# A fourth projection tile by quarters in the opening stage, and expert scratch kept by groups of four blocks and loaded from GpSimd's queue

## The chip, the cores and the metric

The kernel runs on one core of a Trainium2 chip. The metric is the device time of one execution in microseconds (us). All arithmetic is fp32; a product of two fp32 matrices is made of three matmuls on a high and a low half of each factor (hi x hi, hi x lo, lo x hi), and the halves are made on the chip.

## The reference

One layer of a decoder runs on 576 tokens: a prompt of 512 and 8 samples of 8. Width is 2048. Cut to what matters here:

```python
mod = (silu(c) @ w_ada + b_ada).reshape(n, 6, 2048)          # shift1, scale1, gate1, ...
h = rmsnorm(x, norm1_g) * (1 + scale1) + shift1
x_lru, y_gate, sc_b, sc_c, sc_x = split(h @ w_in, ...)       # 5 x 1024 columns
xc = causal_dwconv(x_lru, ...);  rec = rglru(xc + b, ...)    # a scan over time
out_lru = rec * gelu(y_gate)
...                                                          # short conv, two norms, w_out
h2 = rmsnorm(x, norm2_g) * (1 + scale2) + shift2
# peer(h2): 8 heads, each takes 16 of 16384 experts for each token
act = gelu(einsum('td,thkd->thk', h2, expert_u[eidx])) * g
x = x + gate2 * einsum('thk,thkd->td', act, expert_v[eidx])
```

## The kernel before, in words

**Stages, in the trace's time.** To 141 us the modulation (`ada_mm`, L189) streams w_ada in pieces of 1 MB and makes h; projections that can already start run between its pieces. To about 330 us the LRU loop makes one tile of 128 columns of x_lru and one of y_gate for each of i = 0 to 7. The short convolution, the output projection, the second norm and the choice of experts follow to about 1206 us. Experts are then taken in two ways: 80 blocks of 128 experts are computed densely for all tokens, and picks outside these blocks are gathered row by row. In the U stage (1210 to 2205 us) `u_half` multiplies h2 with the blocks (pu, L1400), gelu gives act, and act is written to DRAM scratch `actd`. Beside it the weights of the picks are spread into tiles `stg` by block and token and written to scratch `gd` (L1613). In the V stage (2205 to 3165 us) `v_column` (pv, L1423) multiplies weighted acts with the blocks' rows of V: 80 steps of 4 columns, 12 matmuls each.

**The opening stage.** w_ada comes in for four chunks hc of 512 columns, shift and scale each, and one chunk of the gate: 36 pieces. Modulating a chunk makes a quarter of h's rows, and `first(q, j)` multiplies a sixth of the work of quarter q: tiles x0, x1 (columns 0 and 1 of x_lru) and y0, two halves j of each, 12 matmuls a half. One half stands behind each ada piece from kq == 3 of the next chunk's shift to the end of its scale; the sixth stands at the start of the chunk after that. After the last ada piece (gate, chunk 0) 7 halves are left, and then the loop projects x2, y1, x3, ... with `project`, 96 matmuls each (L139). The order on PE is as written by hand; on other engines a scheduler sets it.

**Scratch.** L = 80 blocks are used in 20 groups sg of SG = 4. `gd[c, partition, block, token]` holds 16 chunks c of 32 tokens; a group needs, in each partition, 16 runs of 4 x 32 floats (512 B). `actd[block, partition, token]` gives a group 4 runs of 2048 B. `load_weights(sg, q)` brings in a quarter of a group's weights (tile gsb, 256 KB) and `load_group` its acts (tile actr, 1 MB), all on ScalarE's queue. `weigh` multiplies them on VectorE (L1352), `halve` makes ahi on ScalarE (L1370) and alo on VectorE (L1374). gsb and actr have one buffer each, so a load waits for the weigh (gsb) or alo (actr) of the group before.

**What sets the order in the V stage.** A table `jobs` hands these out by column: with h_ the column of a group's ahi and hi_at that of the group before (16 columns earlier), the gsb quarters stand at hi_at to hi_at + 3, the actr load at hi_at + 5, weigh at h_ - 3, alo at h_ + 2. SyncE's queue brings in the V blocks (raw, L914, 256 KB), ScalarE makes xhi (L925) and GpSimd xlo (L926) of them. GpSimd also gathers a row of V for each of 128 tokens at a time (v, L1234, 1 MB), up to 5 ahead of use; VectorE adds it up (accB, L1290) and adds the finished columns (acc, L1445). Transfers issued on SyncE and ScalarE take turns at eight completion counters (DMAHW0 to 7), those issued on GpSimd at eight others (DMASW0 to 7): each waits until the one before it on its counter has landed.

Of the kernel before, what the change touches and what calls it, by code (L numbers as in the profile page):

```python
# [5 lines left out]
F32 = mybir.dt.float32  # L6
# [10 lines left out]
KD = 16  # L17
NP = 512
# [62 lines left out]
def build(ctx, tc, A, O, dbg=None):  # L81
# [215 lines left out]
        square_sum(x[:, k, :], k, st, "n1")  # L297
    movs = [(lambda k, a=a, b=b: hv[0][:, k, a:b], lambda k, a=a, b=b: hv[1][:, k, a:b]) for a, b in HALVES]
    LX = 3 + NP + NB * (3 + NS)
    p_early = [pp.tile([128, 2, 512], F32, name=f"pp_x{i}", tag="pp") for i in range(2)]  # L300
    w_early = {}

    def first_weights(q):

        for i, (src, tags) in enumerate(((A["w_in"][1], ("xp", "xc", "hs")), (A["w_in"][KW], ("tr", "ti", "e"))), 1):
            raw, hi, lo = (wk.tile([128, LX], F32, name=f"w{i}{t}{q}", tag=t, bufs=3 - i)[:, :512] for t in tags)
            nc.sync.dma_start(raw, src[q // 2][:, 4 * (q % 2):4 * (q % 2) + 4, :].rearrange("p k c -> p (k c)"))
            S.activation(hi.bitcast(F32R), raw, AF.Copy)
            G.tensor_sub(lo.bitcast(F32R), raw, hi)
            w_early[i, q] = [x.bitcast(F32R).rearrange("p (k c) -> p k c", c=128) for x in (hi, lo)]  # L310

    def first(q, j):

        i, ks = j // 2, range(4 * q + 2 * (j % 2), 4 * q + 2 * (j % 2) + 2)
        if i == 0:
            mm3([p_early[0][:, 0, :HT], p_early[0][:, 1, :HS]], *w_first, movs, ks)
            return
        if q == 0 and j == 4:
            p_early.append([pst.tile([128, 512], F32, name=f"pp_y0{i}", tag="st") for i in range(2)])
        hi, lo = w_early[i, q]  # L320
        outs = [p_early[2][0][:, :HT], p_early[2][1][:, :HS]] if i == 2 else [p_early[1][:, 0, :HT], p_early[1][:, 1, :HS]]
        for k in ks:
            for st, pick in ((hi, 0), (hi, 1), (lo, 0)):
                for o, mv in zip(outs, movs):
                    PE.matmul(o, st[:, k % 4, :], mv[pick](k), start=k == 0 and st is hi and pick == 0,
                              stop=k == KD - 1 and st is lo)

    def scale_x(q):

# [5 lines left out]
    for hc in range(4):  # L335
        for kq in range(4):
            ada_mm(0, hc, kq)
            if hc == 0 and kq == 2:
                spread = norm_stats(st, D, "n1")
            if hc and kq == 0:  # L340
                for p in parts_left:
                    first(*p)
                parts_left = [(hc - 1, j) for j in range(6)]
            if hc and kq == 3:
                first(*parts_left.pop(0))
        ada_out(0, hc)
        for kq in range(4):
            ada_mm(1, hc, kq)
            if parts_left:
                first(*parts_left.pop(0))  # L350
            if hc == 0 and kq == 0:
                R = spread()
                scale_x(0)
        ada_out(1, hc)
        modulate(x, None, 1, 0, 4 * hc, 4, "h")
        if hc == 0:
            w_first = stream_w(A["w_in"][0], "x0")
            for q in range(1, 4):
                scale_x(q)
        first_weights(hc)  # L360
    for kq in range(4):
        ada_mm(2, 0, kq)
    for p in parts_left + [(3, j) for j in range(6)]:
        first(*p)


# [60 lines left out]
    def wt(n, i, b=1):  # L427
        return wk.tile([128, LX], F32, name=f"{n}{i}", tag=n, bufs=b)

    def lru_conv(i, p):  # L430
        xp = wt("xp", i, 2)
        V.memset(xp[:, 0:3], 0.0)
        V.tensor_copy(smp(xp, SO, 3, 0, 3), cst[:, i, :, :])
        S.activation(xp[:, 3:3 + HT], p[:, 0, :HT], AF.Copy)
        S.activation(xp[:, 3 + HT:3 + NP], p[:, 1, :NX], AF.Copy)
        S.activation(smp(xp, SO, 3, 3, 11), s3(p[:, 1, NX:HS]), AF.Copy)
        V.tensor_copy(st_c[:, i, 0, :], xp[:, NP:NP + 3])
        V.tensor_copy(st_c[:, i, 1:, :], smp(xp, SO, 3, 8, 11))
        xc = wt("xc", i, 2)
        cw = lambda k: cols[:, C_CW + k * KW + i:C_CW + k * KW + i + 1]  # L440
        V.tensor_scalar(xc[:, :LN], xp[:, 0:LN], cw(0), cols[:, C_CB + i:C_CB + i + 1], op0=ALU.mult, op1=ALU.add)
        for k in range(1, 4):
            V.scalar_tensor_tensor(xc[:, :LN], xp[:, k:k + LN], cw(k), xc[:, :LN], op0=ALU.mult, op1=ALU.add)
        xcs[i] = xc
# [56 lines left out]

    def sc_x(i, p):
        c = sc_t[i]
        cx = wk.tile([128, LC], F32, name=f"cx{i}", tag="xp", bufs=2)
        V.memset(cx[:, 0:2], 0.0)
        V.tensor_copy(smp(cx, CO, 2, 0, 2), sst[:, i, :, :])
        V.tensor_mul(cx[:, 2:2 + HT], p[:, 0, :HT], c[:, :HT])
        V.tensor_mul(cx[:, 2 + HT:2 + NP], p[:, 1, :NX], c[:, HT:NP])
        V.tensor_mul(smp(cx, CO, 2, 2, 10), s3(p[:, 1, NX:HS]), s3(c[:, NP:]))
        V.tensor_copy(st_s[:, i, 0, :], cx[:, NP:NP + 2])  # L510
        V.tensor_copy(st_s[:, i, 1:, :], smp(cx, CO, 2, 8, 10))
        cv = wk.tile([128, LC], F32, name=f"cv{i}", tag="xc", bufs=2)
# [17 lines left out]
    def ada_turn(n, keep=7):  # L530
# [4 lines left out]
        for _ in range(min(n, len(todo) - keep)):  # L535
            a = todo.pop(0)
            ada_mm(*a)
            if a[2] == 3:
                pend.append(a[:2])
                break  # L540

    gate_act(0, p_early[2])
    lru_conv(0, p_early[0])
    px = p_early[1]
    for i in range(KW):
        if i + 1 < KW:
            lru_conv(i + 1, px)
        if i + 2 < KW:
            px = project(A["w_in"][i + 2], f"x{i + 2}")
            ada_turn(1)  # L550
        lru_gate(i, 0)
        if i + 1 < KW:
            py = project(A["w_in"][KW + i + 1], f"y{i + 1}")
            gate_act(i + 1, [py[:, a, :] for a in range(2)])
        else:
            ada_turn(1)
            pc0 = project(A["w_in"][24], "c0")
        lru_gate(i, 1)
# [153 lines left out]
    V.tensor_copy(outs, words)  # L712
    V.tensor_sub(words[:, 1:], words[:, 1:], outs[:, :KM - 1])
    pickd = dr.tile([NA, 2 * NPK], F32, name="pickd")
    gd = dr.tile([NCH, 128, L, TC], F32, name="gd")
    actd = dr.tile([L, 128, NA], F32, name="actd")
    accd = dr.tile([NA, D], F32, name="accd")
    accs = dr.tile([128, D], F32, name="accs")
    x2d = dr.tile([128, KD, NA], F32, name="x2d")
# [617 lines left out]
    def load_group(sg):  # L1337

        acts[sg] = ep.tile([128, SG, NA], F32, name=f"actr{sg}", tag="actr", bufs=1)
        nc.scalar.dma_start(acts[sg], actd[real(SG * sg):real(SG * sg) + SG].rearrange("i p t -> p i t"))  # L1340

    def load_weights(sg, q):

        if q == 0:
            gsb[sg] = ep.tile([128, NCH, SG * TC], F32, name=f"gsb{sg}", tag="gsb", bufs=1)
        nc.scalar.dma_start(gsb[sg][:, 4 * q:4 * q + 4, :],
                            gd[4 * q:4 * q + 4, :, real(SG * sg):real(SG * sg) + SG, :].rearrange("c p i t -> p c (i t)"))

    def weigh(sg):

# [39 lines left out]
    def u_half(n, i, c):  # L1390
# [213 lines left out]
    def g_out(b, pg):  # L1604
# [5 lines left out]
        if b0 == TC // 4 - 1:  # L1610
            full = stg.pop(c)
            for q in range(0, L, L // 4):
                puts.append(lambda q=q: nc.scalar.dma_start(gd[c][:, q:q + L // 4, :], full[:, q:q + L // 4, :]))  # L1613

    def put(n):
        for f in puts[:n]:
# [28 lines left out]
    for n in range(NU2):  # L1645
# [61 lines left out]
        if n - E0 == 2:  # L1707
            load_group(0)
        for sg, o in ((0, 1), (1, 7)):
            if 0 <= n - E0 - o < 4:  # L1710
                load_weights(sg, n - E0 - o)
        if n - E0 == 6:
            weigh(0)
        if n - E0 == 7:
# [25 lines left out]
    for sg in range(2, L // SG):  # L1740
        use = uses_of[sg * SG]
        free = KQ * (uses_of[(sg - 3) * SG][-1] + 1) if sg >= 3 else 0
        h_ = min(KQ * use[0] - 7, max(free, hi_at + 16))
        assert h_ >= free and h_ >= hi_at + 13, (sg, h_, free, hi_at)
        for j in range(4):
            jobs.setdefault(max(hi_at + j, j), []).append(lambda sg=sg, j=j: load_weights(sg, j))
        jobs.setdefault(max(hi_at + 5, 0), []).append(lambda sg=sg: load_group(sg))
        jobs.setdefault(h_ - 3, []).append(lambda sg=sg: weigh(sg))
        jobs.setdefault(h_, []).append(lambda sg=sg: halve(sg, 0))
        jobs.setdefault(h_ + 2, []).append(lambda sg=sg: halve(sg, 1))  # L1750
        hi_at = h_
# [204 lines left out]
```

## Time and profile before

| what | us |
| --- | --- |
| three runs | 3232.68, 3227.56, 3228.02 (median 3228.02) |
| the profiled execution | 3220.77, its span 3218.9 |
| PE busy | 3040.3 (94%) |
| DVE, POOL, ACT busy | 2216.1, 1730.1, 1039.3 |
| opening stage / U stage / V stage | 0 to 141 / 1210 to 2205 / 2205 to 3165 |

Engines are PE (TensorE), PEld (its weight loads), DVE (VectorE), ACT (ScalarE), POOL (GpSimd) and SP (SyncE). q1 and q10 are the queues of transfers issued by SP and by ACT, q0 that of POOL. A row of waits reads: who waited, for whom, total us, times, longest. A row of windows reads: start and end, length, busy time and instructions of PE, PEld, DVE, ACT and POOL, the granted TensorE clock, the busy share of the 16 DMA engines, GB/s.

### The profile page before, as it was taken

How to read it: one execution, taken by the hardware profiler on the slowest of the kernel's cores; microseconds unless marked ns; L12 is line 12 of the kernel's file. 1: busy time of each engine (PE TensorE's matmuls, PEld its weight loads, DVE VectorE, ACT ScalarE, POOL GpSimd, SP SyncE). 2: the span in 40 equal slices, each digit the busy share in tenths (PEclk: the TensorE clock that was granted, in tenths of full speed). 3: DMA queues.
4: the chain of work that ended last, by engine and by line, in shares of the span. 5: the costliest groups of instructions: out<-in, count | busy, mean ns of one | idle time of the engine just before them, and what ended most of it. 6: DMA issues, size and time to landing. Idle time of an engine off the chain costs nothing.

```text
span 3218.9 us, 52798 instructions
## 1 busy us (share of the span) xinstructions
PE 3040.3 (94%) x20313; PEld 2567.7 (80%) x20313; DVE 2216.1 (69%) x3296; ACT 1039.3 (32%) x1645; POOL 1730.1 (54%) x994
## 2 busy tenths in 40 slices
PE   5999999999989999999999999999999999989997
PEld 2688798899979898887888888877877877777776
DVE  5355521234355797988998998876777897778855
ACT  3243311123232223232656555622222122122122
POOL 2233233344333335666566666666777777577742
PEclk8999999999989999999999999999999999999998
DMA  9834465633332226989879998999999997999964
GB/s 370 300 133 139 156 217 204 210 114 117 130 134 101 73 73 215 314 325 370 340 304 385 389 403 346 372 368 364 399 392 391 389 349 280 357 346 362 363 211 147
DMA packets 300786, 881.13 MB, mean 274 GB/s; under 512 B 37190, under 2 KB 79046, under 8 KB 249062
## 3 DMA queue, kind: packets, MB, share of 16 engines
q1 hardware_dynamic: 161760, 382.48, 33.7%
q0 software_dynamic: 66336, 413.41, 32.4%
q10 hardware_dynamic: 72432, 81.80, 7.3%
q8 instruction: 160, 2.62, 0.3%
q14 instruction: 98, 0.80, 0.1%
HBM read 878.84 MB, written 65.76 MB: 293 GB/s over the span
## 4 chain that ended last, share of the span: by engine, by line
PE 68%; DMA 18%; DVE 6%; issue 3%; POOL 3%; ACT 1%; SPq 0%; ACTq 0%; POOLq 0%; DVEq 0%
PE pu L1400 24%; PE pv L1423 10%; DMA gsb<-gd 7%; PE pp_o L139 6%; DMA actr<-actd 5%; PE pp_s L139 3%; PE pp_c L139 3%; PE pp_x L139 3%; PE qb L139 3%; PE pp_b L139 3%; DMA raw<-vq 3%; PE ada L189 3%; PE pp_y L139 2%; PE qa L139 2%; DMA wa<-w_ada 2%
## 5 line engine op out<-in xcount | busy, mean ns | idle before, releaser
L926 POOL TENSOR_TENSOR xlo<-raw,xhi 128x1024 fp32r<-128x1024 f32 x320 | 786.7, 2467 | 421.4 <-ACT xhi L925 410.3
L925 ACT ACTIVATE xhi<-raw 128x1024 fp32r<-128x1024 f32 x320 | 337.7, 1060 | 856.0 <-PE pv L1423 291.8
L1262 DVE SCALAR_TENSOR_TENSOR u<-u,hT 128x2048 f32<-128x2048 f32 x223 | 504.9, 2283 | 111.7 <-DMA u<-u,rows 111.4
L1290 DVE SCALAR_TENSOR_TENSOR accB<-v,dots,accB 128x2048 f32<-128x2048 f32 x211 | 496.5, 2353 | 114.3 <-DMA v<-v,rows 111.6
L1423 PE MATMUL pv<-ahi,xhi 128*128 128x512 f32 x1280 | 510.4, 399 | 46.0 <-DVE acc L1445 37.4
L1423 PE MATMUL pv<-ahi,xlo 128*128 128x512 f32 x1280 | 507.2, 396 | 15.2 <-POOL xlo L926 15.2
L1400 PE MATMUL pu<-hhi,xhi 128*128 128x512 f32 x1280 | 507.2, 396 | 0.7 <-ACT qt L949 0.7
L1423 PE MATMUL pv<-alo,xhi 128*128 128x512 f32 x1280 | 506.4, 396 | 1.2 <-DVE alo L1374 1.2
L1400 PE MATMUL pu<-hhi,xlo 128*128 128x512 f32 x1280 | 499.5, 390 | 4.8 <-POOL xlo L926 4.8
L1400 PE MATMUL pu<-hlo,xhi 128*128 128x512 f32 x1280 | 499.5, 390 | 0.0
L1423 PEld LDWEIGHTS pv<-ahi,xhi 128*128 128x128 f32 x1280 | 245.2, 192 | 105.5 <-issue 23.1
L1234 POOL DMA_INDIRECT u<-u,rows x223 | 224.7, 1007 | 172.4 <-DVE u L1262 124.9
L1234 POOL DMA_INDIRECT v<-v,rows x223 | 271.6, 1218 | 61.9 <-issue 39.0
L1423 PEld LDWEIGHTS pv<-ahi,xlo 128*128 128x128 f32 x1280 | 245.1, 191 | 72.4 <-POOL xlo L926 20.4
L1400 PEld LDWEIGHTS pu<-hhi,xhi 128*128 128x128 f32 x1280 | 240.7, 188 | 58.0 <-issue 1.7
L1400 PEld LDWEIGHTS pu<-hhi,xlo 128*128 128x128 f32 x1280 | 240.6, 188 | 57.9 <-POOL xlo L926 7.2
L1423 PEld LDWEIGHTS pv<-alo,xhi 128*128 128x128 f32 x1280 | 245.1, 192 | 51.7 <-DVE alo L1374 1.6
L1400 PEld LDWEIGHTS pu<-hlo,xhi 128*128 128x128 f32 x1280 | 240.7, 188 | 47.6
L1595 ACT ACTIVATE op<-op,it 128x128 f32<-128x128 f32 x512 | 155.4, 391 | 2.0 <-issue 0.9
L128 POOL TENSOR_TENSOR wlo_q<-raw_q,whi_q 128x1024 fp32r<-128x1024 f32 x28 | 68.0, 2431 | 149.0 <-ACT whi_q L126 149.0
L189 PE MATMUL ada<-wa,cpad 128*32 128x512 f32 x768 | 108.7, 663 | 40.1 <-DMA wa<-w_ada 40.0
L128 POOL TENSOR_TENSOR wlo_o<-raw_o,whi_o 128x1024 fp32r<-128x1024 f32 x32 | 77.7, 2427 | 115.9 <-ACT whi_o L126 115.9
(503 smaller groups left out, 5543.1 us busy)
## 6 DMA issues: line engine op xcount, KB each, us to landing
wa<-w_ada SPq DMA_DIRECT2D x96, 1024.0 KB
raw<-ut SPq DMA_DIRECT2D x160, 512.0 KB
raw<-vq SPq DMA_DIRECT2D x320, 256.0 KB
gd<-stg ACTq DMA_DIRECT2D x64, 320.0 KB
gsb<-gd ACTq DMA_DIRECT2D x80, 256.0 KB
actd<-act ACTq DMA_DIRECT2D x76, 256.0 KB
actr<-actd ACTq DMA_DIRECT2D x19, 1024.0 KB
raw_o<-w_out SPq DMA_DIRECT2D x32, 512.0 KB
```

The lines of the kernel that those rows point to most:

```text
L128: lo_engine(share).tensor_sub(lo, raw, r32(hi))
L139: PE.matmul(o, st, mv[pick](k), start=first, stop=last)
L189: PE.matmul(acc[32 * g:32 * g + 32, :], cpad[:, 4 * kq + g, :], w[:, g, :], start=kq == 0, stop=kq == 3)
L925: S.activation(hi, raw, AF.Copy)
L926: G.tensor_sub(lo, raw, r32(hi))
L1234: G.indirect_dma_start(out=out, out_offset=None, in_=src, in_offset=bass.IndirectOffsetOnAxis(ap=idx, axis=0), bounds_check=NE * 128 - 1, ...
L1262: V.scalar_tensor_tensor(r, r, 1.0, st["h"], op0=ALU.mult, op1=ALU.mult, accum_out=dots[i][:, j:j + 1])
L1290: V.scalar_tensor_tensor(st["a"], r, dots[i][:, j:j + 1], st["a"], op0=ALU.mult, op1=ALU.add)
L1400: PE.matmul(pu, st[:, kk, :], movA[mv](k), start=k == 0 and a == 0, stop=k == KD - 1 and a == 2)
L1423: PE.matmul(pv, st, mv, start=first and j == 0 and a == 0, stop=last and not end and j == SG - 1 and a == 2)
L1595: S.activation(ops[:, j0 + j, :], ops[:, j0 + j, :], AF.Copy, scale=it[2][:, b * 4 + j:b * 4 + j + 1])
```

## The change

**A, the opening stage.** A fourth tile, x2, joins: a quarter has 8 halves. One stands behind every ada piece from kq == 3 on into the next chunk, so that after the last piece 3 + 8 = 11 are left. The x2 weights come in by quarters of 256 KB on SyncE (tags w3r, w3h, w3l) ahead of the following ada pieces. The first 256 columns of x0 and x1 share one PSUM bank and those of y0 and x2 another; `clear` zeroes each with one matmul, and ScalarE copies them out (`both`) at the loop's start. The loop no longer projects x2: y1 comes first, and `lru_in` (copies out of PSUM) is cut from `lru_conv`.

**B, the scratch.** gd is laid out as [group][partition][chunk][4 x 32 tokens] and actd as [group][partition][block][token]: a group is 8192 B in one run in each partition. Each is loaded by one 1 MB transfer on GpSimd's queue, gsb at hi_at and actr at hi_at + 4; weigh moves to h_ - 2. The stores of gd (64 of 320 KB on ScalarE's queue) now consist of runs of 512 B instead of 2560 B; those of actd keep runs of 2048 B.

```diff
+    def clear(bank):
+        PE.matmul(bank, ident, none.to_broadcast([128, 512]), start=True, stop=False)
...
-        for i, (src, tags) in enumerate(((A["w_in"][1], ("xp", "xc", "hs")), (A["w_in"][KW], ("tr", "ti", "e"))), 1):
+        for i, (src, tags, b) in enumerate(((A["w_in"][1], ("xp", "xc", "hs"), (3, 2, 2)), (A["w_in"][KW], ("tr", "ti", "e"), (1, 1, 1)),
+                                            (A["w_in"][2], ("w3r", "w3h", "w3l"), (2, 1, 1))), 1):
...
-            if hc and kq == 0:
-                for p in parts_left:
-                    first(*p)
-                parts_left = [(hc - 1, j) for j in range(6)]
             if hc and kq == 3:
+                parts_left = [(hc - 1, j) for j in range(8)]
+            if parts_left:
                 first(*parts_left.pop(0))
...
-    for p in parts_left + [(3, j) for j in range(6)]:
+    for p in parts_left + [(3, j) for j in range(8)]:
...
+    for i, bank in ((0, pe_[1][:, 0, :]), (2, p_yx)):
+        both = wk.tile([128, 512], F32, name=f"both{i}", tag="w3r", bufs=2)
+        S.activation(both, bank, AF.Copy)
...
-        if i + 2 < KW:
+        if i and i + 2 < KW:
             px = project(A["w_in"][i + 2], f"x{i + 2}")
             ada_turn(1)
...
-    gd = dr.tile([NCH, 128, L, TC], F32, name="gd")
-    actd = dr.tile([L, 128, NA], F32, name="actd")
+    gd = dr.tile([L // SG, 128, NCH, SG * TC], F32, name="gd")
+    actd = dr.tile([L // SG, 128, SG, NA], F32, name="actd")
...
-        nc.scalar.dma_start(acts[sg], actd[real(SG * sg):real(SG * sg) + SG].rearrange("i p t -> p i t"))
-    def load_weights(sg, q):
-        if q == 0:
-            gsb[sg] = ep.tile([128, NCH, SG * TC], F32, name=f"gsb{sg}", tag="gsb", bufs=1)
-        nc.scalar.dma_start(gsb[sg][:, 4 * q:4 * q + 4, :],
-                            gd[4 * q:4 * q + 4, :, real(SG * sg):real(SG * sg) + SG, :].rearrange("c p i t -> p c (i t)"))
+        G.dma_start(acts[sg], actd[real_sg[sg]])
+    def load_weights(sg):
+        gsb[sg] = ep.tile([128, NCH, SG * TC], F32, name=f"gsb{sg}", tag="gsb", bufs=1)
+        G.dma_start(gsb[sg], gd[real_sg[sg]])
...
-        for j in range(4):
-            jobs.setdefault(max(hi_at + j, j), []).append(lambda sg=sg, j=j: load_weights(sg, j))
-        jobs.setdefault(max(hi_at + 5, 0), []).append(lambda sg=sg: load_group(sg))
-        jobs.setdefault(h_ - 3, []).append(lambda sg=sg: weigh(sg))
+        jobs.setdefault(max(hi_at, 2), []).append(lambda sg=sg: load_weights(sg))
+        jobs.setdefault(hi_at + 4, []).append(lambda sg=sg: load_group(sg))
+        jobs.setdefault(h_ - 2, []).append(lambda sg=sg: weigh(sg))
```

The first place is PE in the opening stage, at the shift pieces kq = 1 to 3 of chunk 3 (wa_3_1 to wa_3_3, four matmuls a row). Before, these pieces follow one another, and the first half of the next quarter (x0, tile pp_x) comes behind the last:

```order
L189 MATMUL ada_3_655<-wa_3_1_674,cpad 32x512 x4
L189 MATMUL ada_3_655<-wa_3_2_680,cpad 32x512 x4
L189 MATMUL ada_3_655<-wa_3_3_686,cpad 32x512 x4
L139 MATMUL pp_x_164<-hhi,whi_x_1_291 128x256
L139 MATMUL pp_x_164<-hhi,whi_x_1_291 128x320
```

After, a half of the x2 tile (12 matmuls with weights w3h and w3l; its outputs are printed as pp_y_432 and pp_y_433, the banks it shares) stands behind the first of these pieces, and another behind the second:

```order
L189 MATMUL ada_3_701<-wa_3_1_720,cpad 32x512 x4
L340 MATMUL pp_y_432<-hhi,w3w3h_490 128x256
L340 MATMUL pp_y_433<-hhi,w3w3h_490 128x320
L340 MATMUL pp_y_432<-hlo,w3w3h_490 128x256
L340 MATMUL pp_y_433<-hlo,w3w3h_490 128x320
L340 MATMUL pp_y_432<-hhi,w3w3l_491 128x256
L340 MATMUL pp_y_433<-hhi,w3w3l_491 128x320
```

Pieces that had nothing behind them have a half behind them now; a chunk has eight halves between its pieces where it had six.

The second place is POOL in the V stage, at the first pass over the gathers (v_30 to v_35). Before:

```order
L1234 DMA v_30_22726<-v,rows_8671 128x2048
L926 TENSOR_TENSOR xlo_22745<-raw_22465,xhi_22744 128x1024
L926 TENSOR_TENSOR xlo_22749<-raw_22563,xhi_22748 128x1024
L1234 DMA v_31_22783<-v,rows_8671 128x2048
L1234 DMA v_32_22820<-v,rows_8671 128x2048
L926 TENSOR_TENSOR xlo_22841<-raw_22572,xhi_22840 128x1024
L926 TENSOR_TENSOR xlo_22845<-raw_22653,xhi_22844 128x1024
L1234 DMA v_33_22866<-v,rows_8671 128x2048
L1234 DMA v_34_22885<-v,rows_8671 128x2048
L1234 DMA v_35_22918<-v,rows_8671 128x2048
```

After:

```order
L1265 DMA v_30_22732<-v,rows_8690 128x2048
L957 TENSOR_TENSOR xlo_22752<-raw_22475,xhi_22751 128x1024
L957 TENSOR_TENSOR xlo_22756<-raw_22570,xhi_22755 128x1024
L1265 DMA v_31_22790<-v,rows_8690 128x2048
L1376 DMA gsb_22798<-gd 128x2048
L1265 DMA v_32_22826<-v,rows_8690 128x2048
L957 TENSOR_TENSOR xlo_22846<-raw_22579,xhi_22845 128x1024
L957 TENSOR_TENSOR xlo_22850<-raw_22660,xhi_22849 128x1024
L1265 DMA v_33_22871<-v,rows_8690 128x2048
L1265 DMA v_34_22889<-v,rows_8690 128x2048
L1371 DMA actr_22894<-actd 128x2048
L1265 DMA v_35_22922<-v,rows_8690 128x2048
```

The two loads of a group have come into POOL's row between the gathers: gsb ahead of gather 32, actr ahead of gather 35. The same loads before, on ACT:

```order
L1443 ACTIVATE acc<-pv_12_22676 128x512
L1370 ACTIVATE ahi_22788<-actr_22599 128x2048
L1346 DMA gsb_22791<-gd 128x4x128
L1443 ACTIVATE acc<-pv_13_22694 128x512
L1346 DMA gsb_22791<-gd 128x4x128
L1443 ACTIVATE acc<-pv_14_22713 128x512
L1346 DMA gsb_22791<-gd 128x4x128
L1443 ACTIVATE acc<-pv_15_22731 128x512
L925 ACTIVATE xhi_22840<-raw_22572 128x1024
L925 ACTIVATE xhi_22844<-raw_22653 128x1024
L1346 DMA gsb_22791<-gd 128x4x128
L1340 DMA actr_22903<-actd 128x4x512
```

After, ACT's row in the V stage has no transfer in it, only xhi, ahi and the first columns' acc.

More of the change, by code (lines that the diff above doesn't have):

```diff
@@ L299, in build @@
     LX = 3 + NP + NB * (3 + NS)
-    p_early = [pp.tile([128, 2, 512], F32, name=f"pp_x{i}", tag="pp") for i in range(2)]
+    pe_ = [pp.tile([128, 2, 512], F32, name=f"pp_x{i}", tag="pp") for i in range(2)]
+    p_early = [(pe_[1][:, 0, HT * i:HT * i + HT], pe_[0][:, i, :HS]) for i in range(2)]
     w_early = {}
+    none = c1.tile([128, 1], F32, name="none")
+    V.memset(none, 0.0)
+    def clear(bank):
+        PE.matmul(bank, ident, none.to_broadcast([128, 512]), start=True, stop=False)
     def first_weights(q):
-        for i, (src, tags) in enumerate(((A["w_in"][1], ("xp", "xc", "hs")), (A["w_in"][KW], ("tr", "ti", "e"))), 1):
-            raw, hi, lo = (wk.tile([128, LX], F32, name=f"w{i}{t}{q}", tag=t, bufs=3 - i)[:, :512] for t in tags)
+        for i, (src, tags, b) in enumerate(((A["w_in"][1], ("xp", "xc", "hs"), (3, 2, 2)), (A["w_in"][KW], ("tr", "ti", "e"), (1, 1, 1)),
+                                            (A["w_in"][2], ("w3r", "w3h", "w3l"), (2, 1, 1))), 1):
+            raw, hi, lo = (wk.tile([128, LX if i < 3 else 512], F32, name=f"w{i}{t}{q}", tag=t, bufs=c)[:, :512] for t, c in zip(tags, b))
             nc.sync.dma_start(raw, src[q // 2][:, 4 * (q % 2):4 * (q % 2) + 4, :].rearrange("p k c -> p (k c)"))
@@ L310, in first_weights @@
             w_early[i, q] = [x.bitcast(F32R).rearrange("p (k c) -> p k c", c=128) for x in (hi, lo)]
+    p_yx = None
     def first(q, j):
+        nonlocal p_yx
         i, ks = j // 2, range(4 * q + 2 * (j % 2), 4 * q + 2 * (j % 2) + 2)
-        if i == 0:
-            mm3([p_early[0][:, 0, :HT], p_early[0][:, 1, :HS]], *w_first, movs, ks)
-            return
+        if q == 0 and j == 0:
+            clear(pe_[1][:, 0, :])
         if q == 0 and j == 4:
-            p_early.append([pst.tile([128, 512], F32, name=f"pp_y0{i}", tag="st") for i in range(2)])
-        hi, lo = w_early[i, q]
-        outs = [p_early[2][0][:, :HT], p_early[2][1][:, :HS]] if i == 2 else [p_early[1][:, 0, :HT], p_early[1][:, 1, :HS]]
+            a, b = [pst.tile([128, 512], F32, name=f"pp_y0{i}", tag="st") for i in range(2)]
+            p_early.extend([(a[:, :HT], pe_[1][:, 1, :HS]), (a[:, HT:2 * HT], b[:, :HS])])
+            clear(a)
+            p_yx = a
         for k in ks:
[L323 to L326, printed above, removed]
+            if i:
+                wh, wl = (w[:, k % 4, :] for w in w_early[i, q])
+            else:
+                wh, wl = (w[k // 8][:, k % 8, :] for w in w_first)
+            for st, pick in ((wh, 0), (wh, 1), (wl, 0)):
+                for z, (o, mv) in enumerate(zip(p_early[i], movs)):
+                    PE.matmul(o, st, mv[pick](k), start=z == 1 and k == 0 and st is wh and pick == 0,
+                              stop=k == KD - 1 and st is wl and z + i % 2 > 0)
     def scale_x(q):
@@ L428, in wt, with lru_in, lru_conv @@
         return wk.tile([128, LX], F32, name=f"{n}{i}", tag=n, bufs=b)
-    def lru_conv(i, p):
-        xp = wt("xp", i, 2)
+    xps = {}
+    def lru_in(i, p):
+        xps[i] = xp = wt("xp", i, 3)
         V.memset(xp[:, 0:3], 0.0)
         V.tensor_copy(smp(xp, SO, 3, 0, 3), cst[:, i, :, :])
-        S.activation(xp[:, 3:3 + HT], p[:, 0, :HT], AF.Copy)
-        S.activation(xp[:, 3 + HT:3 + NP], p[:, 1, :NX], AF.Copy)
-        S.activation(smp(xp, SO, 3, 3, 11), s3(p[:, 1, NX:HS]), AF.Copy)
+        S.activation(xp[:, 3:3 + HT], p[0][:, :HT], AF.Copy)
+        S.activation(xp[:, 3 + HT:3 + NP], p[1][:, :NX], AF.Copy)
+        S.activation(smp(xp, SO, 3, 3, 11), s3(p[1][:, NX:HS]), AF.Copy)
+    def lru_conv(i):
+        xp = xps.pop(i)
         V.tensor_copy(st_c[:, i, 0, :], xp[:, NP:NP + 3])
@@ L503, in sc_x @@
         c = sc_t[i]
-        cx = wk.tile([128, LC], F32, name=f"cx{i}", tag="xp", bufs=2)
+        cx = wk.tile([128, LC], F32, name=f"cx{i}", tag="xp", bufs=3)
         V.memset(cx[:, 0:2], 0.0)
@@ L540, in ada_turn @@
                 break
+    for i, bank in ((0, pe_[1][:, 0, :]), (2, p_yx)):
+        both = wk.tile([128, 512], F32, name=f"both{i}", tag="w3r", bufs=2)
+        S.activation(both, bank, AF.Copy)
+        for j in range(2):
+            p_early[i + j] = both[:, j * HT:j * HT + HT], p_early[i + j][1]
+    lru_in(0, p_early[0])
+    lru_in(1, p_early[1])
     gate_act(0, p_early[2])
-    lru_conv(0, p_early[0])
-    px = p_early[1]
+    lru_in(2, p_early[3])
+    lru_conv(0)
     for i in range(KW):
+        if 1 < i < KW - 1:
+            lru_in(i + 1, [px[:, a, :] for a in range(2)])
         if i + 1 < KW:
-            lru_conv(i + 1, px)
-        if i + 2 < KW:
+            lru_conv(i + 1)
+        if i and i + 2 < KW:
             px = project(A["w_in"][i + 2], f"x{i + 2}")
             ada_turn(1)
-        lru_gate(i, 0)
+        if i:
+            lru_gate(i, 0)
         if i + 1 < KW:
@@ L554, in build @@
             gate_act(i + 1, [py[:, a, :] for a in range(2)])
+            if not i:
+                ada_turn(1)
+                lru_gate(0, 0)
         else:
@@ L1404, in u_half @@
             if i < L - SG:
-                nc.scalar.dma_start(actd[i], act)
+                nc.scalar.dma_start(actd[i // SG, :, i % SG, :], act)
             else:
@@ L1612, in g_out @@
             for q in range(0, L, L // 4):
-                puts.append(lambda q=q: nc.scalar.dma_start(gd[c][:, q:q + L // 4, :], full[:, q:q + L // 4, :]))
+                puts.append(lambda q=q: nc.scalar.dma_start(
+                    gd[q // SG:(q + L // 4) // SG, :, c, :].rearrange("s p x -> p s x"),
+                    full[:, q:q + L // 4, :].rearrange("p (s i) t -> p s (i t)", i=SG)))
     def put(n):
@@ L1709, in build @@
         for sg, o in ((0, 1), (1, 7)):
-            if 0 <= n - E0 - o < 4:
-                load_weights(sg, n - E0 - o)
+            if n - E0 == o:
+                load_weights(sg)
         if n - E0 == 6:
```

## The prediction

> **What bounds the kernel now.** I read the page from the top: engines, slices, then the chain.
>
> ```profile
> PE 3040.3 (94%) x20313; PEld 2567.7 (80%) x20313; DVE 2216.1 (69%) x3296; ACT 1039.3 (32%) x1645; POOL 1730.1 (54%) x994
> DMA  9834465633332226989879998999999997999964
> ```
>
> PE is busy 94% of the span, so all that any edit can win is its idle 6% or matmuls taken away. The DMA engines are full in two places: the first slices and nearly all of the last half. The windows of the opening stage, U and V come next.
>
> ```profile
> 104.00:128.00 24.00, 19.48 (x141) 10.42 (x133) 7.91 (x19) 5.17 (x8) 4.36 (x3) 0.95 1.05 398
> 1550.00:2120.00 570.00, 570.00 (x5969) 461.99 (x5968) 506.04 (x691) 333.76 (x729) 362.89 (x242) 1.00 0.92 364
> 2250.00:3050.00 800.00, 746.84 (x3196) 607.46 (x3196) 644.06 (x358) 177.50 (x166) 585.14 (x342) 0.98 0.97 364
> ```
>
> In U, PE never stops and DMA has 8% to spare. In V, DMA is 97% busy and PE lacks 53 of 800 us: V is where transfers set the pace. The waits there (2225 to 3080) and the chain say which.
>
> ```profile
> ACT xhi L925 <- DMA raw<-vq: 221.0, 46, 14.6
> POOL xlo L926 <- ACT xhi L925: 163.4, 54, 12.7
> DVE accB L1290 <- DMA v<-v,rows: 107.3, 58, 8.8
> PE pv L1423 <- DVE acc L1445: 37.4, 14, 7.5
> DVE actr L1352 <- DMA actr<-actd: 32.2, 6, 9.8
> PE pv L1423 <- POOL xlo L926: 13.5, 10, 2.7
> SPq L914 <- DMA gsb<-gd: 345.4, 45, 19.4
> 2185.85 26.65 DMA gsb<-gd
> 2314.18 25.89 DMA actr<-actd
> 2831.83 38.14 DMA gsb<-gd
> ```
>
> PE waits mostly for VectorE's acc, and VectorE for rows of V and for a group's loads. The last wait row is the telling one: SP's loads of V blocks stand 345 us behind gsb loads, because both take turns at the same eight completion counters. So a scratch load that takes 26 to 38 us holds the blocks, these hold xhi, xlo and PE.
>
> **B, the V stage.** Removed in the 800-us window: 68 loads of gsb and 17 of actr on ACT's queue. Added: as many MB on POOL's queue, one transfer each.
>
> ```profile
> q0 software_dynamic: 29751, 186.72, 58.6%
> q1 hardware_dynamic: 37712, 68.67, 24.2%
> q10 hardware_dynamic: 44404, 35.05, 13.9%
> gsb<-gd ACTq DMA_DIRECT2D x68, 256.0 KB
> actr<-actd ACTq DMA_DIRECT2D x17, 1024.0 KB
> v<-v,rows POOLq DMA_INDIRECT x201, 10.8
> ```
>
> q10 carries nothing but these. It takes 13.9% for 35.05 MB, q0 58.6% for 186.72 MB, in runs of 8192 B (a gathered row), as the scratch will be. At q0's price 35.05 MB take 35.05 x 58.6 / 186.72 = 11.0%; 2.9% of 800 us, 23 us of all 16 engines' time, fall away. DMA work goes from 776 to 753 us; PE's 3196 matmuls start 0.228 us apart when nothing holds them (the rows below, five steps in 1.14 us): 729. DMA stays the longer one and V follows it: **-23**. Bounds: 0 if run length is not what made q10 dear, -47 (800 to 753) if DMA's 3% of idleness goes too.
>
> ```profile
> 2204.73 0.39 PE L1423 MATMUL pv<-ahi,xhi 128*128 128x512 f32 x1
> 2205.87 0.39 PE L1423 MATMUL pv<-ahi,xlo 128*128 128x512 f32 x1
> ```
>
> A rule gives the first bound less: the Trainium skill, "DMA: Bandwidth & Descriptors", section "Why small descriptors are slow (HBM only)", has a fixed overhead of some 3 cycles a packet; at the 850 MHz of its section "Where 436 GB/s comes from" 39,000 packets fewer would be an estimated 9 us over 16 engines, and the sum would be 14 us less of a gain. The row's 2.9% is kept, since it is measured on these very transfers.
>
> Part of the idle 3% is of the change's own making: with no transfer of ACT left in V, SP's blocks no longer queue behind gsb or actr at a counter (345 us of waits), and ACT's xhi no longer behind a held issue. Of the idle 24 us I give a quarter, **-6**; 0 if SP then waits for xlo's buffers instead, -24 at most.
>
> What it costs on POOL: an issue like accs<-v, plus the 0.3 us gap that its neighbours show.
>
> ```profile
> L1296 POOL DMA_DIRECT2D accs<-v x1 | 0.6, 582 | 0.0
> L926 POOL TENSOR_TENSOR xlo<-raw,xhi 128x1024 fp32r<-128x1024 f32 x134 | 334.4, 2512 | 154.0 <-ACT xhi L925 152.1 <-DMA raw<-vq 1.1
> ```
>
> 34 loads x 0.9 us = 30 us, inside the 152 us in which POOL stands waiting for xhi; where it is not idle, behind the load are xlo and then PE. I take a tenth: **+3** (0 to +15). The loads wait for VectorE: gsb for the last weigh, actr for the last alo, and gathers and xlo queue behind them. At the place where each load will stand, the weigh or alo is over in the trace in most groups, by some 16 us on average; the closest pair is this:
>
> ```profile
> 2400.68 1.00 POOL L1234 DMA_INDIRECT v<-v,rows  x1 [0.16 <-issue]
> 2403.14 2.29 DVE L1374 TENSOR_TENSOR alo<-actr,ahi 128x2048 fp32r<-128x2048 f32 x1
> ```
>
> There a load would hold POOL from 2401 to 2405.4, 4 us. I sum about 15 us of holds over 34 loads, also inside the 152. Gathers behind a load land up to 3.5 us later (1 MB at 300 to 364 GB/s), with five ahead of use; before, the same bytes ran beside them on another queue, so the rows come no later on the whole. Moving weigh one column on costs nothing while it has been waiting for its loads (32.2 us above).
>
> **B, the start of V.** PE's wait here ends with the first gsb loads:
>
> ```profile
> 2209.83 0.50 PE L1423 MATMUL pv<-ahi,xhi 128*128 128x512 f32 x1 [3.58 <-ACT xhi L925]
> 2212.62 1.29 DVE L1361 TENSOR_TENSOR actr<-act,gsb 128x512 f32<-128x512 f32 x2 [8.75 <-DMA gsb<-gd]
> ```
>
> VectorE waits 8.75 us for group 1's weights, and ACT's xhi stands behind. The chain's 26.65 us for that load becomes one transfer behind a few gathers (10.8 us). **-4**: the 3.58 and some of what follows at a cold clock; 0 to -8, the bound being VectorE's wait.
>
> **B, the stores in U.** 64 stores of 320 KB change from 2560-B to 512-B runs.
>
> ```profile
> q10 hardware_dynamic: 10817, 22.56, 14.4%
> gd<-stg ACTq DMA_DIRECT2D x42, 320.0 KB
> ```
>
> In 1600 to 2000 (rows above) q10 paid 14.4% of 400 us for 22.56 MB, 41 engine-us a MB; in V, mixed 512 and 2048 B, 51; with actr at U's 41 to 45, gsb's own 512-B runs cost about 57. (57 - 41) x 21 MB / 16 = 21 us more DMA work, against 8% of U's 700 us of stores, 56 us. PE has no wait in U to lengthen: **+2** (0 to +15).
>
> **A.** The trace's chain where the pieces end, and the loop's start:
>
> ```profile
> 119.57 6.45 DMA wa<-w_ada
> 126.06 1.93 PE ada L189 x8
> 138.04 3.12 PE pp_y L325 x24
> 141.17 12.80 PE pp_x L139 x96
> 156.56 12.99 PE pp_y L139 x96
> ```
>
> Removed: x2's 12.80 us. Added: two halves' worth of tail twice over, 11 instead of 7, four at 3.12 / 2 = 1.56: 6.2 us. The rest of x2 goes between pieces, where the chain waits for wa anyway. But 1.05 MB of x2 weights now run ahead of the last piece in a stage where DMA is full (share 1.05, 398 GB/s): 2.6 us. Two clears, matmuls of 512 columns as in ada, are 0.5. ACT's copies precede y1's end by more than 6 us in the new order. -12.8 + 6.2 + 2.6 + 0.5 = -3.5, rounded to **-4**. Bounds: -7 if the last piece is not later (the x2 weights then no longer compete in the loop), -1 if the pieces, now a half behind each, also pay PE time where wa came early.
>
> **The sum.** -23 - 6 + 3 - 4 + 2 - 4 = -32 against the profiled 3220.77, which lies 7.3 us under the median of the runs shown, 3228.0. On the median: 3228 - 32 = **3196**.
>
> **Rivals.**
> 1. *The scratch was hidden anyway.* VectorE still waits for rows of V (107.3 us), the gathers share their queue with the scratch, and PE's 37.4 us for acc stay. For it: DVE is busy 644 of 800 us, POOL 585, and both are chained to rows. Against: SP's 345 us and the loads on the chain. Then A and half of V's start remain: 3228 - 6 = 3222, about 3218 to 3232.
> 2. *Slower: POOL held at the loads.* A load that waits for VectorE holds the gathers and xlo behind it. POOL's 152 us of idleness over 34 loads are 4.5 us a load: from there on the hold decides. At 7 us a load, (7 + 0.9) x 34 = 269, less 152 = 117 us of POOL's time. If half of it reaches PE through a late xlo, +58, less the 35 gained in the other terms: 3251. For it: weigh and alo lengthen beside POOL's work, and gathers beside them,
>
> ```profile
> L1352 DVE TENSOR_TENSOR actr<-actr,gsb 128x2048 f32<-128x2048 f32 x16 | 50.9, 3181 | 46.5 <-DMA actr<-actd 32.2 <-DMA raw<-vq 14.2
> 2292.66 5.90 DVE L1352 TENSOR_TENSOR actr<-actr,gsb 128x2048 f32<-128x2048 f32 x1
> 2354.18 2.87 POOL L1234 DMA_INDIRECT v<-v,rows  x1 [0.16 <-issue]
> 2357.36 1.00 POOL L1234 DMA_INDIRECT v<-v,rows  x1 [0.30 <-issue]
> ```
>
> a weigh 5.90 us against a mean of 3.18, a gather 2.87 against 1.00. Against: the load waits for just that weigh or alo, which is then over. The Trainium skill, "SBUF — State Buffer", section "SBUF: two separate sides", warns of this: a transfer issued from GpSimd gets no descriptors while VectorE holds the shared port, and it says to issue from SP or ACT. The trace agrees as far as that one gather goes.
> 3. *More: the pipeline frees itself.* Blocks come early, weighs never wait, V runs at DMA's 753 us: -47 instead of -29, and V's start -8: 3228 - 60 = 3172.
> 4. *U becomes DMA-bound* by the short stores, from the point where they cost more than 8%: +15 and late first loads: 3212.
>
> **How the numbers follow.** My forecast 0.54 (3180 to 3212), rival 1 0.17, rival 2 0.11, rival 3 0.12, rival 4 0.06. A measurement here can tell 0.2%, 6.5 us, from no change: same is 3221.5 to 3234.5. Faster: 0.54 + 0.12 + 0.06 and a third of rival 1, 0.77; same: two thirds of rival 1 and a bit of rival 2's near end, 0.13; slower 0.10. The range 3168 to 3230 leaves out rival 2, the top of rival 1 and the far end of rival 3.
>
> **What would show it.** In V: no transfers on q10, q0's share near 69%, DMA share still 0.95 or more over a V stage some 30 us shorter; no weigh waiting for actr; SP waiting for xlo, not gsb; POOL's waits for VectorE at the loads about 15 us in all. At the start: PE's first wait under 2 us. In U: PE still without idleness, DMA share 0.95. In the opening: 11 halves in 17 us behind the last piece, y1 at about 152.5 instead of 156.56. The prediction is wrong if POOL's loads or gathers show waits for VectorE above 100 us, if accB's waits for rows grow by more than the weighs' shrink, or if the queue's price for scratch on q0 is no lower than it was on q10.

## The result, and the profile after

The changed kernel takes 3241.98 us (median of 6 runs, 3237.29 to 3252.43), the kernel before 3227.79 (6 runs): a ratio of 1.0053, 95% interval 1.0034 to 1.0071. The forecast was 3196, faster; it is slower by half a percent. The profiled execution took 3237.29 (span 3235.5), that of before 3220.77 (span 3218.9): 16.6 us between the spans, and the stages show where. The bounds are the first pu and pv matmuls and the last row of pv in the two traces (in that of before it starts at 3190.8, so V reaches beyond 3165). Two executions at a much lower granted clock, one of the kernel before (3551.95 us, clock 0.80) and one of e3 (8659.67, clock 0.64), are left out of every ratio and range.

| stage, us | before | after | change | forecast |
| --- | --- | --- | --- | --- |
| start of U (all that comes before) | 1209.8 | 1206.4 | -3.4 | -4 |
| U | 994.9 | 1047.4 | +52.5 | +2 |
| V, to its last row of pv | 986.1 | 953.0 | -33.1 | -30 (-23, -6, +3, -4) |

The start of U and V came out near their forecasts. U lost more than both gained. First the page and the windows of after: U's stretch, and 800 us of V.

```profile
PE 3049.9 (94%) x20317; PEld 2574.8 (80%) x20317; DVE 2214.5 (68%) x3297; ACT 1041.5 (32%) x1649; POOL 1737.4 (54%) x1035
1550.00:2170.00 620.00, 585.77 (x5950) 469.96 (x5949) 508.39 (x692) 332.27 (x723) 364.48 (x243) 0.98 0.90 337
2300.00:3100.00 800.00, 766.19 (x3319) 627.42 (x3318) 669.81 (x376) 185.59 (x172) 607.71 (x383) 0.99 0.94 367
```

In V, PE now does 3319 matmuls in 800 us where it did 3196. In U, where the window of before shows no idleness, it is idle for 34 of 620 us, with the DMA share at 0.90, below the 0.92 of before: U isn't short of transfer time on the whole. What PE waits for in U, in the rows of waits, and what ACT does at one such place, in the timeline (ACTq is ACT's issuing of transfers):

```profile
PE gbank L1630 <- ACT stg L1637: 16.2, 3, 8.9
PE gx L1630 <- issue: 11.5, 28, 0.5
PE gx L1630 <- ACT act L1432: 5.9, 1, 5.9
2043.49 11.43 ACTq L1642 DMA_DIRECT2D gd<-stg  x2
2055.02 0.70 ACT L1637 ACTIVATE stg<-gbank 128x320 f32<-128x320 f32 x1 [10.49 <-issue]
2170.40 17.02 DMA gd<-stg
```

Two stores of gd hold ACT's queue for 11.4 us; the copy into stg behind them comes 10.5 us late, and PE's next gbank matmuls wait for it. The last row is from the chain, at the end of U: it now runs through a store. The rows of the store's line in both traces give the issue's duration (smallest, median, largest, ns), 64 stores each:

```profile
L1613 ACTq DMA_DIRECT2D gd<-stg x64: 326/444/1387, 1555.0 to 2117.2; - x64
L1642 ACTq DMA_DIRECT2D gd<-stg x64: 366/616/10516, 1551.6 to 2172.3; - x64
```

V after, in the queues' rows (2300 to 3100), the waits (2275 to 3090) and PE's first wait in the timeline:

```profile
q0 software_dynamic: 34980, 220.95, 68.9%
q1 hardware_dynamic: 39744, 72.37, 25.2%
SPq L945 <- POOL xlo L957: 409.9, 138, 13.5
DVE accB L1321 <- DMA v<-v,rows: 116.3, 82, 5.0
PE pv L1452 <- DVE acc L1474: 27.6, 15, 7.1
POOL gsb L1376 <- DVE actr L1381: 4.5, 2, 2.8
2257.19 0.50 PE L1452 MATMUL pv<-ahi,xlo 128*128 128x512 f32 x1 [1.41 <-POOL xlo L957]
```

q10 is gone and q0 has 68.9%, as forecast; the DMA share is 0.94, where 0.95 or more was expected. SP no longer waits for gsb; it waits for xlo to free its buffers. No weigh waits for actr. POOL's holds at the loads are 4.5 us in all. PE's first wait in V is 1.41 us, where it was 3.58.

### The profile page after: what moved, and what is told of

Read it like the earlier page. It is cut to its first block, busy times and chain, and to the rows that moved or that the text cites. A ratio compares the mean times of both kernels' runs of the same rounds, so it can differ in the third digit from the quotient of the medians.

```text
span 3235.5 us, 52712 instructions
## 1 busy us (share of the span) xinstructions
PE 3049.9 (94%) x20317; PEld 2574.8 (80%) x20317; DVE 2214.5 (68%) x3297; ACT 1041.5 (32%) x1649; POOL 1737.4 (54%) x1035
## 4 chain that ended last, share of the span: by engine, by line
PE 73%; DMA 11%; DVE 7%; issue 3%; POOL 2%; ACTq 1%; ACT 1%; SPq 0%; POOLq 0%; DVEq 0%
PE pu L1429 23%; PE pv L1452 16%; PE pp_o L139 6%; DMA v<-v,rows 4%; PE pp_s L139 3%; PE pp_c L139 3%; PE qb L139 3%; PE pp_b L139 3%; PE ada L189 2%; PE pp_y L139 2%; PE qa L139 2%; DMA raw<-vq 2%; PE pp_x L139 2%; DVE accB L1321 2%; DMA wa<-w_ada 2%
## 5 line engine op out<-in xcount | busy, mean ns | idle before, releaser
L1265 POOL DMA_INDIRECT v<-v,rows x223 | 258.2, 1158 | 67.8 <-issue 42.0
L1432 ACT ACTIVATE act<-pu 128x512 f32<-128x512 f32 x80 | 47.8, 597 | 290.2 <-PE pu L1429 269.5
```

The costliest lines, as they stand in the source:

```text
L1265: G.indirect_dma_start(out=out, out_offset=None, in_=src, in_offset=bass.IndirectOffsetOnAxis(ap=idx, axis=0), bounds_check=NE * 128 - 1, ...
```

## The experiments

The runs e1 to e4, e5 to e8 and e9 to e12 were made together in three groups, each on another chip, where the kernel before took 3228.06, 3214.67 and 3213.08 us; each ratio is against the kernel before of its own group. A U or V given is that of the one profiled execution. How far these lengths vary is shown by one kernel on two chips (e6 and e12: U 999.8 and 1002.1, V 952.7 and 946.9) and by e4, whose V, with nothing of V edited, is 6.5 us under that of before. So V's differences of 6 us between groups tell nothing.

One theory after the result: the stores' 512-B runs cost U its time. The rivals: part A, the loads on GpSimd's queue, or the transfers' sheer work. And for V's gain: run length, or the freed counters.

**e4_a_only.** Part A's edits alone on the kernel before.

> Part A alone on the kernel before. If A is worth what the changed kernel's stage bounds say, the U stage begins 3.4 us earlier than before (1206.4 against 1209.8), U and V keep the lengths of before (995 and 986 us, to the last pv matmul), and the time is 3 to 4 us below that of the kernel before. Rival: the 3.4 us were a matter of that one profile, and U begins at 1209 or later.

Measured: 3223.01 against 3228.06 (ratio 0.9989, 0.9973 to 1.0005). U starts at 1207.2, V is 979.6. But U is 1008.9, 14 us more than before, with waits that no earlier profile had:

```profile
PE gx L1632 <- issue: 9.4, 23, 0.5
```

The gain of 3 us was there, the length of U was not as expected. The waits turn up in the profiles of e1 to e4, which ran together, and in that of after, and in none of e5 to e12; see the last section.

**e1_old_gd.** The changed kernel with the old layout of gd.

```diff
-    gd = dr.tile([L // SG, 128, NCH, SG * TC], F32, name="gd")
+    gd = dr.tile([NCH, 128, L, TC], F32, name="gd")
-        G.dma_start(gsb[sg], gd[real_sg[sg]])
+        G.dma_start(gsb[sg], gd[:, :, real(SG * sg):real(SG * sg) + SG, :].rearrange("c p i t -> p c (i t)"))
...
+                puts.append(lambda q=q: nc.scalar.dma_start(gd[c][:, q:q + L // 4, :], full[:, q:q + L // 4, :]))
```

> The changed kernel with gd as before ([chunk][partition][block][token]): its 64 stores are 2560-B runs again, and a group's weights still come as one 1 MB transfer on GpSimd's queue, now of 512-B runs. Theory 1 (the stores' five times as many packets are what U lost): U is back from 1047 to 995 to 1000 us. V: if the 33 us won came from freeing the eight counters and ACT's queue, V stays at 953 to 960; if they came from the saved transfer work, of which only the acts' 5 us are left, V is about 975 to 980. Time 3228 - 4 - 30 = 3194 by the first, 3215 by the second. Rival (U was lost to the loads on GpSimd's queue or to part A): U stays near 1047.

Measured: 3212.45 (0.9958, 0.9943 to 0.9973), U 1010.3, V 969.3. U is that of e4, which holds the old stores too: the stores' layout cost 37 us (1047.4 less 1010.3; 39 against e3, of the same group), and the loads on GpSimd's queue cost U nothing. V lies between the two values expected.

**e2_spaced.** `put(1)` for `put(2)`.

> The changed kernel with at most one store of gd issued in each half of the U stage instead of two (put(1) for put(2)): same packets, same bytes. Theory 1a (a burst of stores fills ACT's queue, and ScalarE stands until it drains): ACT's issue time for gd falls from 116 us to under 50, U from 1047 to about 1005 to 1015. Theory 1b (a store of 640 packets costs that issue time whatever stands before it) and theory 2 (the transfer engines run out of time in U): U stays within 10 us of 1047.

Measured: 3217.58 (0.9964, 0.9951 to 0.9978), U 1031.2, V 952.2. ACT's issues of the stores take 38 us in all instead of 98 (their durations in the trace of after sum to 97.8, not to the 116 expected), as theory 1a has it, but U got back only 16 us, between the two theories. The standing had moved to what is issued behind them on ACT's queue, the writes of act:

```profile
2046.53 8.48 ACTq L1434 DMA_DIRECT2D actd<-act  x1
2055.11 1.06 ACT L956 ACTIVATE xhi<-raw 128x1024 fp32r<-128x1024 f32 x1 [8.61 <-issue]
```

In the stretch in which stores are issued these writes take 56 us to issue here, 28 in after and 15 before. With the stores ACT's queue is held 94 us here, 125 in after and 45 before. SP's loads of U blocks also wait 81 us for stores at a shared counter, where they waited 5.

**e3_loads_act.** `G.dma_start` replaced by `nc.scalar.dma_start` in load_group and load_weights.

> The changed kernel with both loads of a group on ACT's queue again, one transfer of 1 MB in 8192-B runs each, at the new places. U keeps its 1047 us. V: if the saved transfer work made V's gain, V stays near 955 to 960; if the freed counters and ACT's queue made it, V returns to 975 to 985. Time about 3242 by the first, 3265 by the second.

Measured: 3239.35 (1.0035, 1.0011 to 1.0058), U 1049.5, V 947.3. V's whole gain is there with both loads on ACT's queue and the eight counters shared as before. Its queues (2300 to 3100):

```profile
q0 software_dynamic: 30082, 185.29, 57.5%
q10 hardware_dynamic: 4896, 35.65, 11.3%
```

**e5_stores_sp.** The stores on SP's queue (`nc.sync.dma_start` in puts).

> The changed kernel with the 64 stores of gd issued on SP's queue instead of ACT's: same packets, bytes and places. Theory 1 (U lost its 37 us to ScalarE standing at the issue of these stores, with stg and xhi behind them): U falls from 1047 to 1005 to 1015, the issue time moves to SP, and V keeps its 953: about 3205. Theory 2 (transfer engines or DRAM are too slow for 512-B stores): U stays above 1035. Rival 3: SP now stands instead, its loads of the U blocks (raw) come late and PE waits for xhi: U 1020 to 1040.

Measured: 3238.3 against 3214.67 (1.0071, 1.0046 to 1.0096), U 1045.0, V 945.2. ACT issues no store and U is as long. PE's waits in U: a copy into stg comes late, and PE waits for it.

```profile
PE pu L1429 <- ACT stg L1637: 30.0, 8, 12.8
PE gbank L1630 <- ACT stg L1637: 9.3, 4, 5.1
DMA to landing us min/median/max: 5.3/17.7/27.4
```

The third row is from the store's line, from issue to landing, of the 35 stores whose landing the trace has; e8, the kernel before, has 4.7/14.6/18.9 for nine. stg has two buffers, but no late store held one of them here: by the packets in the trace, a chunk's stores had all ended 17 us or more before the first copy into the same buffer. The timeline shows another reason, first on SP, then on ACT, then on PE; the last two rows are ACT's waits for U blocks, before (1550 to 2205) and here (1550 to 2250):

```profile
1757.44 21.82 SPq L940 DMA_DIRECT2D raw<-ut  x4
1769.20 1.06 ACT L956 ACTIVATE xhi<-raw 128x1024 fp32r<-128x1024 f32 x1 [10.58 <-DMA raw<-ut]
1770.16 0.71 ACT L1637 ACTIVATE stg<-gbank 128x320 f32<-128x320 f32 x1
1771.49 0.50 PE L1429 MATMUL pu<-hhi,xhi 128*128 128x512 f32 x1 [2.63 <-ACT stg L1637]
ACT xhi L925 <- DMA raw<-ut: 30.0, 9, 7.6
ACT xhi L956 <- DMA raw<-ut: 134.8, 23, 19.5
```

Now SP stands: in the stretch of the stores its issues of them take 120 us and those of the U blocks among them 173, where those took 29 before. The blocks come late, ACT's xhi waits for them, the copies into stg stand behind xhi in ACT's order, and PE waits for the copies. That is rival 3 of the expectation, at a higher price. Theory 1 falls as far as it names ScalarE; what it says of the engine that issues stays.

**e6_stores_pool.** The stores on GpSimd's queue (`G.dma_start` in puts).

> The changed kernel with the stores of gd on GpSimd's queue, among the gathers. Theory 1: U falls to 1005 to 1020, since POOL has idle time in U; the gathers behind a store land later and VectorE waits more for rows of u. Rival: 640 packets a store written by GpSimd cost it more than its idle time, xlo comes late and U stays at 1030 or more.

Measured: 3187.3 (0.9901, 0.9880 to 0.9923), U 999.8, V 952.7. The same stores into the same layout cost U 5 us instead of 45. The rows of the store's line, and of the window's queues (1550 to 2120):

```profile
L1642 POOL DMA_DIRECT2D gd<-stg x64: 860/914/943, 1553.9 to 2125.7; - x64
DMA to landing us min/median/max: 7.1/10.7/12.6
q0 software_dynamic: 27443, 149.96, 65.7%
q10 hardware_dynamic: 6345, 11.55, 5.3%
```

POOL issues a store in 0.91 us, and the ten landings that the trace has come after 10.7 us, the latest after 12.6. No write of act and no U block takes more than 0.4 us to issue. Where 40,960 packets of 512 B left ACT's queue, the trace of e6 has packets of 4096 B on q0 (5216 of them in U, 96 of which stand there before too): the trace lists eight runs as one packet.

**e7_old_gd_act.** e1 with both loads on ACT's queue.

> Run e1 with both loads of a group on ACT's queue: gd in the old layout with 512-B load runs, actd in the new one, one transfer each. Beside e1 (V 969) it shows what GpSimd's queue alone is worth in V, beside e3 (V 947) what the length of gsb's runs is worth. If the queue matters (freed counters), V is 980 or more; if only run lengths and the number of transfers do, V is 965 to 972. U as in e1, 1010.

Measured: 3202.74 (0.9957, 0.9934 to 0.9981), U 999.5, V 963.7. The queue alone is worth nothing that shows in V (e1 969.3, this 963.7); gsb's run length is worth 16 us (963.7 against e3's 947.3 with the loads on ACT's queue, e1's 969.3 against after's 953.0 with them on GpSimd's). Its q10 (2250 to 3050) costs what that of before did:

```profile
q10 hardware_dynamic: 37536, 35.65, 13.7%
SPq L945 <- DMA gsb<-gd: 235.1, 12, 30.5
```

SP stands at gsb for 235 us here, and V is shorter than before by 22 us all the same.

**e8_before.** The kernel before, once more.

> The kernel before, unchanged, for a second profile of it. Its 27 times so far lie between 3217 and 3233 us, and the first profile (3220.8) is among the low ones; the two kernels that hold part A and the old stores had 23 waits of 0.4 us in the gx matmuls of U, 9.4 us, and U of 1009 to 1010 us. If these waits belong to single executions, they turn up here with a time above 3225; if they belong to part A, this profile has none and U is 995.

Measured: 3220.82, U 994.0, V 988.1, no waits at gx. The profile of before was no chance: U and V are within 2 us of it.

**e9_stores_two.** The four stores of a chunk in turn on ACT's and SP's queue.

```diff
-                puts.append(lambda q=q: nc.scalar.dma_start(
+                puts.append(lambda q=q: (nc.sync if q % (L // 2) else nc.scalar).dma_start(
```

> The changed kernel with the four stores of a chunk issued in turn on ACT's and on SP's queue. In runs e3 and e5 each 512-B run was a packet of its own on these queues, in e6 the same stores went out from GpSimd in 4096-B packets, and U was 1045 to 1050 there and 1000 here. Theory 4 (a queue gets one packet a turn on each transfer engine, so 40 packets a store and engine wait 40 turns): with two queues a chunk's 160 turns run side by side, the stores land earlier, and U falls to 1015 to 1030. Rival (the stores' bytes or DRAM's handling of 512-B runs set the time, whatever the queue): U stays at 1045.

Measured: 3212.63 against 3213.08 (1.0000, 0.9986 to 1.0013), U 1021.7, V 953.4. With two queues half of the loss is gone, in the range that theory 4 gave; the bytes and their 512-B runs are the same. Its reason is not borne out: a store lands after 3.7/19.1/28.8 us here, no earlier than in e5. No issue of a store takes longer than 1.5 us now, and the U blocks on SP's queue take 59 us to issue, where e5 has 173; but ACT's xhi still waits 131 us for them, and PE for stg (16.2 and 11.0 us):

```profile
L1642 SPq DMA_DIRECT2D gd<-stg x32: 382/405/1504, 1543.9 to 2134.4; - x32
L1642 ACTq DMA_DIRECT2D gd<-stg x32: 377/377/775, 1549.7 to 2142.0; - x32
```

**e10_b_pool, e11_pool_act, e12_pool_again.** e6 without part A; e6 with the loads on ACT's queue; e6 again.

> Part B alone with the stores on GpSimd's queue (run e6 without part A): U starts at 1208 to 1210 instead of 1205 to 1206, U is 995 to 1000, V 953; the time is 2 to 4 us above run e12 of this call. Rival: A costs as much elsewhere as it saves, and the two are equal.

> Run e6 with the loads of gsb and actr on ACT's queue, stores on GpSimd's. V followed the transfer engines' work in all runs so far (share 0.96), and that is the same here: V 945 to 955, time within 6 us of e12. If the eight counters that SP and ACT share cost something, V is 960 or more.

> Run e6 again, on this call's chip: U 1000 and V 953 again, about 27 us (0.9%) under the kernel before.

Measured, against 3213.08: e10 3187.74 (0.9927, 0.9902 to 0.9952), e11 3181.88 (0.9903, 0.9882 to 0.9923), e12 3186.35 (0.9917, 0.9898 to 0.9937). U starts at 1210.2 without A and at 1206.2 and 1205.5 with it; U is 1000 to 1002 and V 945 to 947 in all three. A's 4 to 5 us at U's start are plain in the traces and too small for the times (1.4 us, inside the intervals). The lowest median is that of e11 (both parts, loads on ACT's queue, stores on GpSimd's), about 1% under the kernel before; its interval overlaps those of e10 and e12.

## Why the prediction was wrong, point by point

**The step that failed: "B, the stores in U", +2 (0 to +15).** It priced the stores as transfer work only. That work was sized about right: in the U window q10 went from 14.2% of 570 us to 15.7% of 630, 81 to 99 us, +18 where 21 was forecast, and the DMA share even fell. What it left out is the issue: "PE has no wait in U to lengthen" looked at PE alone and took the engine that issues as free. With 640 packets instead of 128 in a store, the issues of stores and of acts hold ACT for 125 us where they held it for 45, up to 10.5 us at a time. ACT's copies into stg and its xhi stand behind the issue in ACT's order, and PE behind the copies. With the stores on SP's queue the same happens by way of the U blocks (e5). U lost 37 us (after against e1, both with the waits at gx) to 45 us (e5 against e6, both without). The other 14 or so of the 52 go with the waits at gx, which are themselves 9 to 12 us: e4 has them, and a U 14 us longer, with the old stores, and e6 and e7 hold part A without them.

**Rival 4** had the right place, the short stores, and the wrong mechanism and size: it asked for U to become short of DMA time, at +15. U was not; its share was 0.90.

**What makes them slow.** Shown: not the layout or the bytes (e6: 1000), not ScalarE as the one that issues (e5: 1045), but many short packets on one hardware queue, whose issuing engine then stands (e9, two queues: 1022; e2, spaced: 1031). A buffer of stg held by a late store is not it: by the packets in the traces, a chunk's stores end at least 14.5 us before the first copy into the same buffer in before, 6.6 in after, 17.0 in e5 and 16.8 in e9; only e2, which spaces them out, comes closer, to 0.4. The trace's packets take 27 ns for 512 B, 103 for 2560, 171 for 4096 and 320 to 331 for 8192 (a gathered row). A store needs 40 short packets from each of the 16 engines instead of 8. The Trainium skill, "DMA: Bandwidth & Descriptors", section "Queues, rings and completion order", says that an engine goes round its queues and drains a whole packet, of several descriptors, from one of them before it switches. Theory 4 took one 512-B packet for a turn, so that each would stand behind about one gathered row. The traces do not agree with that: while stores drained, 0.90 gathered rows moved for each packet of 2560 B before, and 0.21 for each packet of 512 B in after, so about five short packets to a row. Why an issue stands was not measured by itself; in after the issues of over 1.5 us for a store all come with 640 or more packets of that queue still to move.

**"B, the V stage", -23 - 6 + 3, and V's start, -4: right in sum, one term wrong, and the sum in part luck.** The -23 is borne out by e3, which changes run length and keeps the queue: q10 falls from 13.9% for 35.05 MB to 11.3% for 35.65, against 11.0% forecast. Summed over V's packets (V less its first 20 and last 110 us) the 16 engines work 822 us before, 803 in e7, 781 in after, 779 in e3, 778 in e11; that work is 0.946 to 0.961 of the stretch in every run, so V follows the transfers' work. The -6 for the freed counters was wrong: e3 and e11 share the counters and have V 947 and 945, after, e10 and e12 free them and have 953, 946 and 947, and SP's wait for gsb turned into a wait for xlo. In its place the rest of the work grew cheaper, for reasons that no run singles out: from before to after q1 went from 218 to 208 us, and the gathers from 327 to 324 ns each; e4, with V unedited, has 6.5 us of this too. The fixed overhead of a packet that the prediction took from the Trainium skill ("DMA: Bandwidth & Descriptors", "Why small descriptors are slow (HBM only)") would have had an estimated 9 us for the saved work; q10's share of 800 us measured 111 us before and 90 in e3, 21 less. POOL's cost was 0.58 us a load and 4.5 us of holds in all, where 15 were counted. The Trainium skill's warning about transfers issued from GpSimd, the one that rival 2 named ("SBUF — State Buffer", "SBUF: two separate sides"), is not seen at these loads: none took more than 0.61 us to issue.

**"A", -4: right.** The eleven profiles with A start U at 1204.7 to 1207.9, the three without at 1208.0 to 1210.2; the nearest two, e5 and e8, are 0.1 apart. Its parts, in the chain of after:

```profile
130.82 1.94 PE ada L189 x8
139.10 6.40 PE pp_x L340 x48
151.89 12.80 PE pp_y L139 x96
```

The last piece ends 4.8 us later than before (2.6 forecast), the halves take the 1.6 us expected, and y1 starts at 151.9 (152.5 forecast), 19 us behind the last piece where 17 were expected.

**The range** ended at 3230, since the transfers whose runs were made five times shorter were given +15 at most; they cost 37 to 45. (In rival 3's sum, 3228 - 60 is 3168, not 3172.)

## What to carry to other kernels

A layout has two sides: a run that is made long for the load is made short for the store. Price the store by its packets and by the queue that carries them, and ask what is issued behind it on that queue and what the issuing engine has to do next, before saying that it hides in spare transfer time. Moving such a store to another engine's queue moves the standing with it (e5), and spacing it out moves it to the next transfer (e2). Where a stage's transfers fill the engines, its length follows their work: there run length pays whichever engine issues them. And issuing a short-run store from GpSimd was worth 45 us here, where the trace has eight runs in a packet.

## What the runs showed of the hardware that was not expected

With stores of 640 packets on it, an issue on ACT's queue took up to 10.5 us (after) or 13.2 (e3), and one on SP's up to 12.3 (e5); with 128 packets a store, no issue of a store took over 1.9 (before and e8).

GpSimd's queue made 4096-B packets out of 512-B runs, in stores (e6) and in loads (e1's gsb on q0: 4608 packets of 4096 B in V), where ACT's and SP's queues made one packet of each run.

In five profiles PE stood 23 to 28 times for about 0.4 us inside the gx matmuls of U, 9.4 to 11.5 us in all, with no releaser shown: after, and e1 to e4, all of which hold part A. In each of them the waits come again at about the 590th, 815th, 942nd, 1164th, 1388th and 1967th of the 2048 gx matmuls. e5, e6, e7, e9, e11 and e12 hold it too and have none. They ran at other times, so it seems to go with the chip or the execution and not with the edit; what it is stays open, and so does whether executions without a profile have it. The times of e4, 3214 to 3232, lie like those of the kernel before beside it, 3217 to 3231.
